# Three embedding blocks and sixteen idle products at the start of a hybrid encoder step, and one store on another queue

## The chip, the core and the metric

The kernel runs on one core of a Trainium2 chip. The metric is the time of one launch on the device in microseconds (us), lower is better. TensorE (PE in the profile) multiplies matrices, VectorE (DVE), ScalarE (ACT) and GpSimd (POOL) work element by element, and SyncE (SP) issues most of the transfers.

## The reference

One inference step of a one-layer encoder on 1024 prompt rows and 32 decode rows, all in float32, `D_MODEL` 1024. Cut to what is computed:

```python
h = rmsnorm(x, g_mix)
q, k, v, cb, cc, cx, ga, gc = jnp.split(h @ w_in, SPLITS, axis=-1)
y_attn = attend(q, k, v).reshape(b, t, SB_WIDTH) @ w_attn_out   # stick-breaking, 8 heads x 64
conv_out, new_buf = causal_conv(cc * cx, conv_buf, conv_w)      # width 3, 512 channels
y_conv = (cb * conv_out) @ w_conv_out
x = x + (sigmoid(ga) * y_attn + sigmoid(gc) * y_conv) @ w_o
x = x + square(relu(rmsnorm(x, g_ffn) @ w_up)) @ w_down         # 4 * D_MODEL wide
x = x + sigmoid(rmsnorm(x, g_ple) @ w_ple_gate) * (p @ w_ple)   # p: 256 features per row
y = rmsnorm(x, g_final)
```

The term `p @ w_ple`, the embedding, hangs on no other part of the step: its inputs are `p` (1056 x 256) and `w_ple` (256 x 1024).

## The kernel before

Activations lie feature-major: a block is 128 features by T = 1056 rows (1024 prompt, 32 decode). Each f32 product is made of three fp32r products: a tensor is cast to a high part on ScalarE (`h`), and the low part is the difference, on VectorE (`l`); TensorE adds high x high, high x low and low x high in one PSUM group.

The stages in order:

1. *Loads and first gates.* Two gate weights (`raw_i`) and the input `xf` are loaded on SyncE's queue. `first_gates` makes the first four gate blocks in 16 groups of 24 products, 264 columns each (`products`, lines 202 to 204). `prepare_plain` casts the weights (`load_w`, lines 97 and 98), `parts_x` makes the high and low parts of the scaled input (lines 328 and 141).
2. *Input projections.* Twelve more sets by a seven-product scheme (`seven`): gates 4 to 9, then cc, cx, cb, q, k, v twice. What follows a set (`follow`) runs as side generators beside the next set. For `cb` that is `conv_gate`: it casts the gated convolution to `cvh` on ScalarE (line 567), stores it to `cvd` (line 568), subtracts for the low part (570) and stores that (571).
3. *Attention.* 64 steps of 128 queries each: eight heads (p, j), with eight steps i = 0 to 7 over a growing key length of 128 (i + 1). A step has scores (`scores`, TensorE lines 799 and 800, sigmoid on ScalarE, masking on GpSimd), a running product on VectorE (`left_over`, line 817), transposes on TensorE with copies out by ScalarE and subtractions by VectorE (`flip`, lines 853 to 857), and every second step the sum over values (`gather`, line 872). The steps are staggered over four loop turns in the hand-written `ORDER`. Between them TensorE is given *filler units*: gates 10 to 15 (four units each, `gate_unit` and `last_gates`), then the eight embedding blocks (one unit each, `embed_unit`, 18 products with three column slices of 352; the last two blocks are cut otherwise). START = 6 units run ahead of the attention, FILL in it.
4. *Branch projections, merge, output projection, MLP, embedding gate and final norm.*

`pace` spreads FILL over the steps. Each step has a load of the other engines, an `own` time of TensorE, and the filler is what lies between them; four times 1.25 are added for splitting the embedding's inputs (`p_parts`) and weights (`embed_weights`):

```python
unit = (FILL * 2.92 + sum(own)) / sum(load)
part = [max(0.0, unit * v - o) for v, o in zip(load, own)]
part = [x * FILL / sum(part) for x in part]
...
load[next(n for n, e in enumerate(ends) if e > FILL - 11 + more)] += 1.25
```

Inside the blocks of `tc.manual_schedule(engines=MM)` the order on TensorE, VectorE, ScalarE and GpSimd is the order in which the code issues; SyncE's order is chosen by the framework. Blocks of T columns share one pool of 34 buffers (`blk`), raw weights a pool of four (`wraw`).

Of the kernel before, what the change touches and what calls it, by code (L numbers as in the profile page):

```python
# [9 lines left out]
F32 = mybir.dt.float32  # L10
F32R = mybir.dt.float32r
# [4 lines left out]
P = 128  # L16
D = 1024
KD = D // P
# [18 lines left out]
TW = 400  # L37
# [1 line left out]
AT1 = (5, 4, 6, 7, 8, 12)  # L39
AT_IN = (4, 8, 10, 12, 14, 18)  # L40
EARLY_GATES = 10
FILL = 26.0
ORDER = "LSAFBFG"
START = 6
MM = {mybir.EngineType.Activation, mybir.EngineType.PE, mybir.EngineType.DVE, mybir.EngineType.Pool}
# [3 lines left out]
def tile_step(  # L49
# [8 lines left out]
    nc = tc.nc  # L58
# [229 lines left out]
            )  # L288

    near_, far_, whole_ = slice(0, TQ), slice(TQ, TH), slice(0, TH)  # L290
    n_ = base["g"]
    raws["i0"] = [raw_w(w_in, n_, KD, "i0_0")]
    load_x(0, near_)
# [24 lines left out]
    rs = blk("rs")  # L318
    ssq = cpool.tile([P, 9], F32, name="ssq")
    rst = cpool.tile([P, 9], F32, name="rst")  # L320

    def parts_x(h, c, fs=(0, 2, 4, 6, 1, 3, 5, 7)):
        for f in fs:
# [236 lines left out]
    def conv_gate(nb, m):  # L560
        scaled(m)
        yield
        dve(m, m, cst.pop(("y", nb)), op=ALU.mult)
        for _ in range(8 if nb % 2 else 3):
            yield
        h = blk(f"cvh{nb}", F32R)
        nc.scalar.copy(h, m)
        nc.sync.dma_start(cvd[nb, 0], h.bitcast(F32))
        yield
        dve(m.bitcast(F32R), m, h.bitcast(F32), op=sub)  # L570
        nc.sync.dma_start(cvd[nb, 1], m)
        yield
# [17 lines left out]
    def first_gates():  # L590

        m, late = [blk(f"sg{n}") for n in range(2)], []

        def out(s_, i, t):
            p_ = late.pop(0)
            r = m[2 * s_ + i]
            nc.scalar.copy(r[:, quarters[t]], p_)
            if t == (3, 1)[s_]:
                nc.sync.dma_start(gd[2 * s_ + i], r)

        order = [(0, i, t) for t in range(4) for i in range(2)]
        order += [(1, i, t) for h in ((2, 3), (0, 1)) for i in range(2) for t in h]
        for n, (s_, i, t) in enumerate(order):
            if n == 0:
                prepare_plain("i0", 0)
                parts_x(0, near_)
                prepare_plain("i0", 1)
            elif n in (1, 3):
                parts_x(n // 2, far_ if n == 1 else whole_)
            elif n == 8:  # L610
                m.extend(blk(f"sg{n}") for n in (2, 3))
            w, c = ws[f"i{s_}"], t // 2 + 1
            a, b = (("A11", "A12"), ("A21", "A22"))[i]
            late.append(products(f"g{s_}{i}{t}", ((w[a], f"B1{c}"), (w[b], f"B2{c}")), quarters[t % 2]))
            if n:
                out(*order[n - 1])
            if n + 1 == len(order):
                out(*order[n])
            if n == 4:
                side.append(sums_x())  # L620
            elif n in (6, 7):
                prepare_plain("i1", n - 6)
            elif n == 8:
                fetch_in(2)
                side.append(prepare("i2"))
            elif n == 12:
                fetch_in(3)
            yield
# [76 lines left out]

    def p_fetch():
        for i in range(2):
            pwr.append(wraw.tile([P, 4, 2, P], F32, tag="raw", name=f"raw_pw{i}"))
            nc.sync.dma_start(pwr[i], w_ple[:, 4 * i : 4 * i + 4])
        for f in range(2):  # L710
            praw.append(blk(f"pr{f}"))
            nc.sync.dma_start(praw[f], pT[f])
# [4 lines left out]
        pl.append(l)  # L717

    def embed_weights(i):
        h, l = (blk(f"pw{i}{x}", F32R, [P, 4, 2, P]) for x in "hl")  # L720
        nc.scalar.copy(h, pwr[i])
        dve(l, pwr[i], h.bitcast(F32), op=sub)
        pw.append((h, l))

    def embed_unit(n):


        def body(w):
            if 3 <= n < 7:
                conv_parts(n - 3)  # L730
            wh, wl = (x[:, n % 4] for x in pw[n // 4])
            e = blk(f"em{n}")
            cols = ts if n < KD - 2 else tt[:2]
            for c in cols:
                ps = group(f"ps_pw{n}{c.start}", c.stop - c.start)
                for k in range(2):
                    nc.tensor.matmul(ps, wh[:, k, :], ph[k][:, c], start=k == 0, stop=False)
                    nc.tensor.matmul(ps, wh[:, k, :], pl[k][:, c], start=False, stop=False)
                    nc.tensor.matmul(ps, wl[:, k, :], ph[k][:, c], start=False, stop=k == 1)
                nc.scalar.copy(e[:, c], ps)  # L740
                if c is cols[-1]:
                    nc.sync.dma_start(ed[n][:, : c.stop], e[:, : c.stop])
                yield 1 / 3
            if n < KD - 2:
                return
            b = n - (KD - 2)
            tb = slice(2 * TW + b * P, 2 * TW + b * P + P)
            wh, wl = (x[:, 2:4] for x in pw[1])
# [12 lines left out]
        return lambda: None, lambda raw: None, body, (0, 1), 1  # L761
# [184 lines left out]
        return load, body  # L946

    units = [gate_unit(n, 1 if n == 13 else 2) for n in range(EARLY_GATES, 14)] + [last_gates(14)]
    units += [embed_unit(n) for n in range(KD)]
    work = feed(units)  # L950
    done = 0

# [11 lines left out]

    with tc.manual_schedule(engines=MM):
        nc.scalar.preload_act_table_set("sqrt_and_others")
        run(first_gates())
        for s_ in range(2, len(SETS)):
            nm, n = SETS[s_]
            if s_ == 2:  # L970
                side.append(after(1, stats_x()))
            elif s_ == 4:
                nc.scalar.preload_act_table_set("sigmoid_and_others")
            if s_ + 1 < len(SETS):
                side.append(prepare(f"i{s_ + 1}", AT_IN))
# [958 lines left out]
```

## Time and profile before

| | |
|---|---|
| median of 3 runs | 1548.17 us (1547.71 to 1549.49) |
| the profiled execution | 1548.24 us |
| its span, first to last instruction | 1546.5 us |
| TensorE busy | 1524.3 us (99%) |
| VectorE busy | 1061.1 us (69%) |
| ScalarE busy | 756.7 us (49%) |
| transfers | 269.10 MB, mean 174 GB/s |

In a timeline row stand the start, the duration, the engine, the line, the operation, out <- in, the shape, the count, and in brackets the idle time ahead of it and what ended it. A wait row has who waited for whom: the total in us, how many times, the longest. A row of the windows has the stretch, its length, the busy time of PE, PEld (weight loads), DVE, ACT and POOL with their counts, the granted clock, the share of DMA and GB/s. The ends of TensorE's products are modelled and overlap the next product, so the rate is read from the distance between starts. A busy share of TensorE is not its share of peak.

### The profile page before, as it was taken

How to read it: one execution, taken by the hardware profiler on the slowest of the kernel's cores; microseconds unless marked ns; L12 is line 12 of the kernel's file. 1: busy time of each engine (PE TensorE's matmuls, PEld its weight loads, DVE VectorE, ACT ScalarE, POOL GpSimd, SP SyncE). 2: the span in 40 equal slices, each digit the busy share in tenths (PEclk: the TensorE clock that was granted, in tenths of full speed). 3: DMA queues.
4: the chain of work that ended last, by engine and by line, in shares of the span. 5: the costliest groups of instructions: out<-in, count | busy, mean ns of one | idle time of the engine just before them, and what ended most of it. 6: DMA issues, size and time to landing. Idle time of an engine off the chain costs nothing.

```text
span 1546.5 us, 29356 instructions
## 1 busy us (share of the span) xinstructions
PE 1524.3 (99%) x11786; PEld 1509.7 (98%) x11786; DVE 1061.1 (69%) x1398; ACT 756.7 (49%) x1384; POOL 344.5 (22%) x290
## 2 busy tenths in 40 slices
PE   8999999999999999999999999999999999999997
PEld 7999999999899999999999999999999999999997
DVE  7544776666678887766577555545577986789856
ACT  6643344443566775333355555555543334434656
POOL 1222332220211115001312222221020221013352
PEclk9999999999999999999999999999999999999999
DMA  6532145544635466234453344344786897583443
GB/s 226 202 115 72 40 177 205 196 146 110 216 106 155 158 228 241 85 136 169 161 190 144 141 152 147 132 146 154 272 310 203 279 334 243 193 280 112 141 134 111
DMA packets 111559, 269.10 MB, mean 174 GB/s; under 512 B 13472, under 2 KB 29216, under 8 KB 111424
## 3 DMA queue, kind: packets, MB, share of 16 engines
q1 hardware_dynamic: 111280, 267.21, 50.6%
q8 instruction: 92, 1.51, 0.4%
q14 instruction: 43, 0.35, 0.1%
q10 hardware_dynamic: 144, 0.03, 0.0%
HBM read 186.46 MB, written 80.73 MB: 173 GB/s over the span
## 4 chain that ended last, share of the span: by engine, by line
PE 91%; DVE 4%; ACT 2%; issue 1%; DMA 1%; POOL 0%; SPq 0%; POOLq 0%; DVEq 0%; ACTq 0%
PE ps_dn L1467 7%; PE ps_dn L1466 7%; PE ps_dn L1468 7%; PE ps_A11u L203 4%; PE ps_A11u L204 4%; PE ps_A11u L202 4%; PE ps_A11i L204 3%; PE ps_A11i L202 3%; PE ps_A11i L203 3%; PE av L872 2%; PE ps_wo L107 2%; PE ps_wo L106 2%; PE ps_wo L108 2%; PE ps_S1u L203 2%; PE ps_S1u L202 2%; PE ps_S1u L204 2%
## 5 line engine op out<-in xcount | busy, mean ns | idle before, releaser
L1467 PE MATMUL ps_dn<-fl,whi_dn 128*128 128x264 f32 x896 | 254.8, 284 | 0.1
L1468 PE MATMUL ps_dn<-fh,wlo_dn 128*128 128x264 f32 x896 | 254.8, 284 | 0.0
L1466 PE MATMUL ps_dn<-fh,whi_dn 128*128 128x264 f32 x896 | 254.7, 284 | 0.0
L1467 PEld LDWEIGHTS ps_dn<-fl,whi_dn 128*128 128x128 f32 x896 | 168.5, 188 | 0.3 <-DVE fl L1375 0.3
L1466 PEld LDWEIGHTS ps_dn<-fh,whi_dn 128*128 128x128 f32 x896 | 168.7, 188 | 0.0
L1468 PEld LDWEIGHTS ps_dn<-fh,wlo_dn 128*128 128x128 f32 x896 | 168.6, 188 | 0.0
L189 POOL TENSOR_TENSOR s_i<-raw_i,raw_i 128x512 f32<-128x512 f32 x30 | 40.7, 1358 | 229.0 <-DVE slS_i L152 196.1
L1359 DVE TENSOR_TENSOR wlo_dn<-raw_dn,whi_dn 128x1024 fp32r<-128x1024 f32 x40 | 71.2, 1780 | 25.7 <-ACT whi_dn L1353 25.6
L817 DVE TENSOR_TENSOR_SCAN r<-r 128x128 f32<-128x128 f32 (+3 forms) x64 | 86.6, 1353 | 2.2 <-POOL r L810 2.0
L1353 ACT CAST whi_dn<-raw_dn 128x1024 fp32r<-128x1024 f32 x40 | 42.1, 1052 | 94.0 <-PE ps_dn L1467 79.7
L189 POOL TENSOR_TENSOR s_u<-raw_u,raw_u 128x512 f32<-128x512 f32 x30 | 44.3, 1476 | 186.6 <-DVE slS_u L152 157.9
L1408 POOL TENSOR_TENSOR c<-c,rs 128x528 f32<-128x528 f32 x16 | 26.7, 1668 | 244.1 <-DVE c L1475 122.5
L1375 DVE TENSOR_TENSOR fl<-mr,fh 128x1056 fp32r<-128x1056 f32 x56 | 69.7, 1246 | 4.1 <-ACT fh L1370 4.1
L810 POOL TENSOR_SCALAR_AFFINE_SELECT r<-r 128x128 f32<-128x128 f32 x64 | 25.9, 406 | 204.7 <-ACT r L803 204.7
L152 DVE TENSOR_TENSOR slS_i<-s_i,shS_i 128x512 fp32r<-128x512 f32 x45 | 35.2, 787 | 51.8 <-ACT shS_i L150 51.7
L202 PE MATMUL ps_A11u<-T,shS_u 128*128 128x264 f32 x240 | 68.5, 285 | 0.0
L202 PE MATMUL ps_A11i<-T,shS_i 128*128 128x264 f32 x240 | 68.5, 285 | 0.0
L204 PE MATMUL ps_A11i<-T,slS_i 128*128 128x264 f32 x240 | 68.4, 285 | 0.0
L203 PE MATMUL ps_A11u<-T,shS_u 128*128 128x264 f32 x240 | 68.4, 285 | 0.0
L204 PE MATMUL ps_A11u<-T,slS_u 128*128 128x264 f32 x240 | 68.3, 284 | 0.0
L203 PE MATMUL ps_A11i<-T,shS_i 128*128 128x264 f32 x240 | 68.2, 284 | 0.0
L857 DVE TENSOR_TENSOR at<-pa,at 128x512 fp32r<-128x512 f32 (+2 forms) x96 | 51.0, 550 | 19.6 <-ACT at L856 18.8
(462 smaller groups left out, 5604.8 us busy)
## 6 DMA issues: line engine op xcount, KB each, us to landing
raw_dn<-in_w_down_dram SPq DMA_DIRECT2D x56, 512.0 KB, 4.8
raw_i<-in_w_in_dram SPq DMA_DIRECT2D x34, 512.0 KB, 4.5
mr<-mdT SPq DMA_DIRECT2D x32, 528.0 KB, 5.7
raw_u<-in_w_up_dram SPq DMA_DIRECT2D x32, 512.0 KB, 3.6
mdB<-m SPq DMA_DIRECT2D x48, 264.0 KB, 2.4
mr<-mdB SPq DMA_DIRECT2D x24, 528.0 KB, 5.9
s<-gd SPq DMA_DIRECT2D x16, 528.0 KB, 5.3
mdT<-ta SPq DMA_DIRECT2D x32, 264.0 KB, 2.1
```

The source lines that it names most:

```text
L189: f()
L202: nc.tensor.matmul(p_, wh[:, k, :], o[:, 0, c], start=new and n == 0, stop=False, **on)
L203: nc.tensor.matmul(p_, wh[:, k, :], o[:, 1, c], start=False, stop=False, **on)
L204: nc.tensor.matmul(p_, wl[:, k, :], o[:, 0, c], start=False, stop=z, **on)
L817: nc.vector.tensor_tensor_scan(rev, rev, rev, 1.0, ALU.mult, ALU.bypass)
L857: nc.vector.tensor_tensor(al, pt[:, :nb, :], ah.bitcast(F32), op=ALU.subtract)
L1353: nc.scalar.copy(hi, dws[u])
L1359: dve(lo, raw, hi.bitcast(F32), op=sub)
L1375: dve(l, mraw.pop(v), opd[v].bitcast(F32), op=sub)
L1466: nc.tensor.matmul(ps, hi[:, j, :], oh, start=j == 0, stop=False)
L1467: nc.tensor.matmul(ps, hi[:, j, :], ol, start=False, stop=False)
L1468: nc.tensor.matmul(ps, lo[:, j, :], oh, start=False, stop=j == NP_ - 1)
```

## The change

Three embedding blocks (n = 0, 1, 2) leave the attention's fillers and are made by a new function, `first_embeds`, ahead of the first gates. Their loads stand ahead of the first gate weight on SyncE's queue: `w_ple` for the three blocks in two pieces and `p` in six column pieces (1.47 MB). Ahead of their 54 products stand WARM = 16 products of `ones` with itself, whose result nobody reads. Their PSUM groups are emptied inside `first_gates`, by ScalarE for the first and third column slice and by VectorE for the second. FILL goes from 26 to 23. The later loads and casts of `w_ple` take the five remaining blocks; `p` is loaded and cast again for them. In `conv_gate` the store of the high part is issued from ScalarE's queue in place of SyncE's. What is computed stays the same.

```diff
-FILL = 26.0
+FILL = 23.0
+FIRST_EMBEDS = 3
+WARM = 16
...
+    NE = FIRST_EMBEDS
+    pw_first = wraw.tile([P, NE, 2, P], F32, tag="raw", name="raw_pw_first")
+    p_first = [blk(f"pf{f}") for f in range(2)]
+    nc.sync.dma_start(pw_first[:, :1], w_ple[:, :1])
+    for c in ts:
+        for f in range(2):
+            nc.sync.dma_start(p_first[f][:, c], pT[f][:, c])
+        if c is ts[0]:
+            nc.sync.dma_start(pw_first[:, 1:], w_ple[:, 1:NE])
     n_ = base["g"]
     raws["i0"] = [raw_w(w_in, n_, KD, "i0_0")]
...
+    def first_embeds():
+
+        wu = gps.tile([P, TW], F32, tag="g", name="warm")
+        for _ in range(WARM):
+            nc.tensor.matmul(wu[:, :P], ones, ones, start=True, stop=True)
+        wh, wl = (blk(f"pwf{x}", F32R, [P, NE, 2, P]) for x in "hl")
+        h, l = ([blk(f"pf{x}{f}", F32R) for f in range(2)] for x in "hl")
+        e = [blk(f"em{n}") for n in range(NE)]
+        late = []
+
+        def low_w(n):
+            dve(wl[:, n], pw_first[:, n], wh[:, n].bitcast(F32), op=sub)
+
+        def out():
+            n, c, ps = late.pop(0)
+            (nc.vector.tensor_copy if c is ts[1] else nc.scalar.copy)(e[n][:, c], ps)
+            if c is ts[-1]:
+                nc.sync.dma_start(ed[n], e[n])
+
+        nc.vector.tensor_copy(wh[:, 0], pw_first[:, 0])
+        low_w(0)
+        for i, c in enumerate(ts):
+            for f in range(2):
+                nc.scalar.copy(h[f][:, c], p_first[f][:, c])
+            if i == 0:
+                nc.scalar.copy(wh[:, 1:], pw_first[:, 1:])
+            for f in range(2):
+                dve(l[f][:, c], p_first[f][:, c], h[f][:, c].bitcast(F32), op=sub)
+            if i == 0:
+                low_w(slice(1, NE))
+            for n in range(NE):
+                ps = group(f"ps_pw{n}_{i}")
+                for k in range(2):
+                    nc.tensor.matmul(ps, wh[:, n, k, :], h[k][:, c], start=k == 0, stop=False)
+                for k in range(2):
+                    nc.tensor.matmul(ps, wl[:, n, k, :], h[k][:, c], start=False, stop=False)
+                for k in range(2):
+                    nc.tensor.matmul(ps, wh[:, n, k, :], l[k][:, c], start=False, stop=k == 1)
+                late.append((n, c, ps))
+        return out
...
-        nc.sync.dma_start(cvd[nb, 0], h.bitcast(F32))
+        nc.scalar.dma_start(cvd[nb, 0], h.bitcast(F32))
...
                 prepare_plain("i0", 0)
-                parts_x(0, near_)
+                for _ in range(NE):
+                    embed_out()
+                parts_x(0, near_, (0, 2, 4, 6))
+                for _ in range(NE):
+                    embed_out()
+                parts_x(0, near_, (1, 3, 5, 7))
                 prepare_plain("i0", 1)
             elif n in (1, 3):
+                if n == 1:
+                    for _ in range(NE):
+                        embed_out()
                 parts_x(n // 2, far_ if n == 1 else whole_)
...
-            pwr.append(wraw.tile([P, 4, 2, P], F32, tag="raw", name=f"raw_pw{i}"))
-            nc.sync.dma_start(pwr[i], w_ple[:, 4 * i : 4 * i + 4])
+            pwr.append(wraw.tile([P, 3, 2, P], F32, tag="raw", name=f"raw_pw{i}"))
+            nc.sync.dma_start(pwr[i][:, 1 - i :], w_ple[:, 3 + 2 * i : 5 + 3 * i])
...
-    units += [embed_unit(n) for n in range(KD)]
+    units += [embed_unit(n) for n in range(NE, KD)]
...
         nc.scalar.preload_act_table_set("sqrt_and_others")
+        embed_out = first_embeds()
         run(first_gates())
```

More of the change, by code (lines that the diff above doesn't have):

```diff
@@ L719, in embed_weights @@
     def embed_weights(i):
-        h, l = (blk(f"pw{i}{x}", F32R, [P, 4, 2, P]) for x in "hl")
-        nc.scalar.copy(h, pwr[i])
-        dve(l, pwr[i], h.bitcast(F32), op=sub)
+        h, l = (blk(f"pw{i}{x}", F32R, [P, 3, 2, P])[:, 1 - i :] for x in "hl")
+        nc.scalar.copy(h, pwr[i][:, 1 - i :])
+        dve(l, pwr[i][:, 1 - i :], h.bitcast(F32), op=sub)
         pw.append((h, l))
@@ L730, in body @@
                 conv_parts(n - 3)
-            wh, wl = (x[:, n % 4] for x in pw[n // 4])
+            wh, wl = (x[:, n - (3 if n < 5 else 5)] for x in pw[n >= 5])
             e = blk(f"em{n}")
@@ L747, in body @@
             tb = slice(2 * TW + b * P, 2 * TW + b * P + P)
-            wh, wl = (x[:, 2:4] for x in pw[1])
+            wh, wl = (x[:, 1:3] for x in pw[1])
             ps = group(f"ps_pt{b}", 2 * P)
```

## The prediction

> **What bounds the kernel now.** I read the page's totals and chain first, then who TensorE waited for, then the timelines of the three places that the change touches: the opening, the first convolution stores, and the attention.
>
> ```profile
> span 1546.5 us, 29356 instructions
> PE 91%; DVE 4%; ACT 2%; issue 1%; DMA 1%; POOL 0%; SPq 0%; POOLq 0%; DVEq 0%; ACTq 0%
> ```
>
> The chain that ended last is TensorE for 91%. Moving TensorE work pays only where it fills a hole, and only if the place it leaves can run shorter. TensorE's waits over the whole run, those of the attention:
>
> ```profile
> PE z L799 <- ACT r L803: 1.0, 2, 0.5
> PE pa L853 <- DVE r L817: 1.0, 2, 0.8
> ```
>
> The attention shows only 2 us of such waits, so today its fillers are paid in full. The largest hole is the opening (start, duration, engine and line):
>
> ```profile
> 0.90 0.17 DVE L75 MEMSET ones<- 128x128 f32 x1 [0.90 <-PEq L1910]
> 1.24 1.96 SPq L286 DMA_DIRECT2D x<-in_xf_dram  x4
> 4.42 1.04 ACT L97 CAST whi_i<-raw_i 128x1024 fp32r<-128x1024 f32 x1 [1.90 <-DMA raw_i<-in_w_in_dram]
> 5.93 0.59 PE L202 MATMUL ps_g<-B,whi_i 128*128 128x264 f32 x1 [5.93 <-ACT B L328]
> 7.18 0.59 PE L203 MATMUL ps_g<-B,whi_i 128*128 128x264 f32 x1 [0.66 <-DVE B L141]
> 10.20 0.42 PE L204 MATMUL ps_g<-B,wlo_i 128*128 128x264 f32 x1
> 10.42 0.32 PE L202 MATMUL ps_g<-B,whi_i 128*128 128x264 f32 x1
> 11.55 0.28 PE L202 MATMUL ps_g<-B,whi_i 128*128 128x264 f32 x1
> 11.67 0.28 PE L203 MATMUL ps_g<-B,whi_i 128*128 128x264 f32 x1
> 12.11 0.39 PE L204 MATMUL ps_g<-B,wlo_i 128*128 128x264 f32 x1 [0.15 <-DVE wlo_i L98]
> ```
>
> TensorE starts at 5.93. Until 10.42 its products stand 0.22 us apart (10.20, 10.42), later 0.12 (11.55, 11.67): the array runs at about half speed for its first 4.5 us. From 5.93 to 11.67 there are 26 products, worth 26 x 0.121 = 3.15 us at full speed, so 12.11 - 3.15 = 8.96 us are lost by 12.11. One wait follows in the same stage:
>
> ```profile
> 33.47 0.39 PE L204 MATMUL ps_g<-B,wlo_i 128*128 128x264 f32 x1 [0.63 <-DVE wlo_i L98]
> ```
>
> That makes 9.6 us.
>
> **The opening, after.** The sixteen products multiply `ones` by itself in plain f32. The nearest rows are nine products of the same form, and two rows of an embedding block:
>
> ```profile
> L390 PE MATMUL pr<-dg,ones x18: 195/275/377, 83.7 to 85.6; 128*128 128x128 f32 x16, 128*128 128x32 f32 x2
> 534.31 0.32 PE L738 MATMUL ps_pw<-p0l,pw0h 128*128 128x352 f32 x1
> 534.96 0.33 PE L739 MATMUL ps_pw<-p1h,pw0l 128*128 128x352 f32 x1
> ```
>
> Nine products are 18 instructions in 1.9 us, two each, 0.11 us apart at full speed. Slowed as in the opening (0.22 / 0.121 = 1.8) one takes 0.20. Sixteen are 32 instructions from 1.2 us on, when `ones` is set. If the slow stretch lasts 4.5 us again (5.93 to 10.42), 22.5 instructions run slowly until 5.7 and 9.5 fast: done at 6.75. If it lasts 3.2 (7.18 to 10.42), done at 6.2; if it outlasts them, at 1.2 + 32 x 0.20 = 7.6. I take 6.75, the longer stretch being the one counted from the first product. The Trainium skill, "TensorE: Matmul & The Clock Gate", Part 1, puts the warm-up at about 3.4 us of activity in a window that runs freely of the kernel's start; by it the slow stretch would end anywhere from 4.6 to 8.0, an estimate from that page, and the sum below would move by -0.5 to +0.9 us. The trace's 3.2 and 4.5 lie inside that.
>
> Three blocks of 18 products follow. Their rows are 0.16 us apart (four steps from 534.31 to 534.96), so 54 x 0.161 = 8.7 us, and the gates begin at 15.45. Do the inputs come in time?
>
> ```profile
> vecT<-in_vecs_dram ACTq DMA_DIRECT2D x1, 26.0 KB, 3.8
> x<-in_xf_dram SPq DMA_DIRECT2D x8, 264.0 KB, 5.4
> 6.00:9.00 3.00, 2.34 (x9) 2.04 (x10) 2.75 (x6) 2.31 (x6) 0.00 (x0) 1.00 1.05 396
> L740 ACT COPY em<-ps_pw x22: 452/454/506, 524.3 to 579.8; 128x352 f32<-128x352 f32 x18, 128x400 f32<-128x400 f32 x4
> 10.70 3.41 ACT L328 ACTIVATE B<-x,vecT 128x264 fp32r<-128x264 f32 x8
> ```
>
> The smallest load took 3.8 us to land, so the first weight block (131 KB) is there by 4.6; the two 180 KB input pieces behind it, at 396 GB/s, by 5.5; with a cast of about 0.45 the first block can run at 6, under the cover of the idle products. The eight new loads move 1.47 MB, 3.8 us at that rate, and take SyncE's queue 8 x 0.49 = 3.9 us of issuing ahead of the first gate weight. All first-stage loads land 3.8 us later, the gate weight at 8.2 (4.42 + 3.8). ScalarE then casts it (1.04), empties three PSUM groups (1.4) and makes eight parts (8 x 0.43); VectorE follows with its eight parts and three copies. Laid end to end the first four parts are ready near 13 and the last near 16, against 15.45 and about 16.9 when they are used (half a group of 24 products later). That cover is some 1 us; if it is gone, 1 us is added. The 0.63 wait at 33.47 comes in a stage where ScalarE and VectorE have moved less than TensorE; I keep 0.3 of it. Sum: 6.75 + 8.7 + 0.3 - 9.6 = **+6.15 us**, bounds +5.3 (6.2, no wait) and +8.4 (7.6, wait kept, inputs 1 us late). The later `ed` stores on SyncE's queue have nothing urgent behind them.
>
> **The convolution store.** In the sets of input projections:
>
> ```profile
> 193.40 1.08 ACT L567 CAST cvh<-m_i 128x1056 fp32r<-128x1056 f32 x1 [2.22 <-DVE m_i L563]
> 196.89 0.38 SPq L568 DMA_DIRECT2D cvd<-cvh  x1
> 196.89 5.33 DMA cvd<-cvh
> 202.31 1.07 ACT L567 CAST cvh<-m_i 128x1056 fp32r<-128x1056 f32 x1 [6.09 <-DMA cvd<-cvh]
> 205.03 0.39 PE L202 MATMUL ps_A11i<-B,whi_i 128*128 128x264 f32 x1 [1.61 <-DVE m_i L248]
> ```
>
> The cast ends at 194.48, but SyncE, busy with earlier work in its order, issues the store at 196.89; it lands 5.33 us later, ScalarE's next cast waits 6.09 us for that buffer, and everything behind the cast, up to TensorE at 205.03, is late by 1.61. Issued from ScalarE's own queue the store goes 2.4 us earlier; 2.4 is more than 1.61, so the whole wait goes: **-1.6 us**. Four issues of about 0.4 us now stand in ScalarE's order ahead of the casts and PSUM copies, an engine that waits 2.2 us in this very row. Bounds: -1.6, and +1.6 should the issues hold up PSUM copies as long again as today's wait.
>
> **The attention, with 23 units.** Three units of 18 products leave: -8.7 us if TensorE stays the bound. The eight-step stretches, one head each (length, then busy TensorE, weight loads, VectorE):
>
> ```profile
> 416.50:442.60 26.10, 26.10 (x211) 24.13 (x209) 17.34 (x24) 13.92 (x38) 3.66 (x8) 1.00 0.36 108
> 442.60:463.60 21.00, 21.00 (x169) 20.46 (x168) 19.52 (x27) 14.48 (x34) 3.37 (x9) 1.00 0.42 119
> 463.60:484.60 21.00, 21.00 (x168) 20.45 (x167) 19.16 (x26) 14.12 (x33) 2.90 (x8) 1.00 0.46 139
> 484.60:508.00 23.40, 23.40 (x187) 22.77 (x186) 18.83 (x26) 14.14 (x33) 2.35 (x8) 1.00 0.47 141
> 508.00:532.10 24.10, 23.97 (x181) 22.71 (x179) 22.16 (x28) 17.74 (x40) 4.78 (x8) 1.00 0.57 190
> 532.10:553.90 21.80, 21.13 (x151) 20.14 (x149) 18.90 (x26) 15.36 (x37) 3.24 (x9) 1.00 0.62 196
> ```
>
> By `pace`'s own formula the units per eight steps go from 4.15, 2.67, 2.67, 2.67, 3.61, 3.61, 2.67, 2.67 (1.26 behind) to 3.75, 2.33, 2.33, 2.33, 3.66, 2.77, 2.33, 2.33 (1.15). At 2.9 us a unit (18 x 0.161) the third and fourth stretches shrink by 1.0 to 20.0 against VectorE's 19.5 and 19.2, the seventh to 20.8. The sixth shrinks by 2.4 to 21.7. It holds the low parts of the embedding's inputs and weights:
>
> ```profile
> 507.83 1.26 DVE L114 TENSOR_TENSOR p0l<-pr,p0h 128x1056 fp32r<-128x1056 f32 x1 [0.22 <-ACT p0h L113]
> 516.54 1.22 DVE L722 TENSOR_TENSOR pw0l<-raw_pw,pw0h 128x1024 fp32r<-128x1024 f32 x1 [0.26 <-ACT pw0h L721]
> ```
>
> `pace` reserves time for these four at units 15 to 18, written as FILL - 11 on; with FILL at 23 that is 12 to 15, while they still run at 15 to 18, since only later units left. So the added time lands mostly in the fifth stretch, and the first cast (1.26, now just ahead of the sixth) moves into the sixth. The weight casts shrink to half and three quarters (0.6 and 0.9 for 1.22 each); the second falls behind step 48, into the seventh. VectorE's sixth stretch: 22.16 + 1.26 - 0.6 - 1.2 = 21.6 by that, up to 22.5 if the last cast stays.
>
> VectorE has left TensorE unhurt with 1.5 us of room in a stretch (21.0 against 19.52). If it needs those 1.5 us, the third, fourth, sixth and seventh stretches fall short by 1.0, 0.7, 2.3 and 0.5: 4.5 us lost. If it needs none, only the sixth is short, by 0.8. I take 2.4, about half way, as no row shows less room than 1.5 and the stretches can lend to each other. Saved: 8.7 - 2.4 = **-6.3 us**, bounds -4.2 and -7.9.
>
> Sum: +6.15 - 1.6 - 6.3 = -1.75 us. The profiled execution took 1548.24 us (span 1546.5 and 1.7 around it), within 0.1 of the median of three runs, 1548.17. Forecast: 1548.24 - 1.75 = **1546.5 us**.
>
> **Rivals.** *The attention pays in full* (chance 0.25): VectorE keeps up with no room to spare, as its waits shrink when TensorE's transposes come sooner, and the opening is at its lower bound: +5.3 - 1.6 - 7.9 = -4.2, 1544.0 us. For it: 17.34 busy of 26.10 in the second stretch. Against it: 92% busy in the third.
>
> *The attention does not shorten* (0.10, the slow side): VectorE's idle time there is its own order (cast of ScalarE, then its subtraction, then the scan), so every stretch keeps its length and TensorE waits where the fillers stood. Then +6.15 - 1.6 = +4.55, 1552.8 us. It decides as soon as less than about 1.5 us is saved. Against it: TensorE busy 21.00 of 21.00, so the length is TensorE's now.
>
> *The idle products open nothing* (0.08): the array stays slow until about 10.4 whatever ran before. They end at 7.6, then 2.8 us of embedding run at half speed, 1.4 lost: +8.4, in sum +0.5, 1548.7 us.
>
> *ScalarE's store waits in its own queue* (0.05): a DMA issue can wait for an earlier transfer, as this row of SyncE's waits in the first 40 us shows:
>
> ```profile
> SPq L88 <- DMA raw_i<-in_w_in_dram: 6.2, 1, 6.2
> ```
>
> On ScalarE such a wait holds the PSUM copies: the 1.6 stays and up to 6.2 less 2.2 is added: 1548.1 to 1552.1 us.
>
> **How the numbers follow.** The forecast has the remaining 0.52. About 0.2% (3.1 us) is what a measurement of this kernel can tell from no change. Faster by more: nearly all of the first rival and a little of the forecast's low end, 0.30. Slower by more: the second rival and the tail of the last, 0.12. Same: 0.58. The range runs from the first rival with the 508 us stretch unhurt (1543.2) to the forecast with opening and attention both near their bad bounds (1548.24 + 8.4 - 1.6 - 4.2 = 1550.8), cut to 1550.6; it leaves out most of the second rival.
>
> **What would show it.** Right: idle products from 1.2 to about 6.8, embedding products 0.16 apart from about 7, gates from about 15.5 without a hole; no 6.09 wait at the second convolution cast and no 1.61 before the next product; the attention shorter by about 6 us, with a few us of new TensorE waits for the scan or the low parts, most of them near the sixth stretch. Wrong: embedding products 0.3 apart, gates starting after 16.5, a ScalarE wait at the store, or an attention as long as before.

## The result and the profile after

The changed kernel takes 1552.87 us (median of 10 runs, 1551.89 to 1553.5) against 1548.26 (10 runs, 1547.71 to 1550.32) for the kernel before in the same comparison: ratio 1.0027, 95% interval [1.0017, 1.0037]. The forecast was 1546.5 with a range up to 1550.6, so the change is slower where a gain of 1.75 us was expected, and outside the range. Its profiled execution took 1553.01 us, 4.77 more than the 1548.24 of before.

The page's span, and the chain that ended last (shares by engine):

```profile
span 1551.3 us, 29450 instructions
PE 90%; DVE 5%; ACT 2%; issue 1%; DMA 1%; POOL 0%; SPq 0%; DVEq 0%; POOLq 0%; ACTq 0%
```

TensorE still carries the chain. Where the 4.8 us arose is read from the starts of the same products in both timelines. The table gives for every kernel of this study how much later (+) or earlier (-) than in the kernel before, in us, the named product started in the profiled execution.

| kernel | first input set | first scores | attention's last `av` | second branch (`ps_oa`) | first `ps_pg` | last `ps_pg` | end |
|---|---|---|---|---|---|---|---|
| before, at | 56.72 | 392.09 | 586.36 | 631.14 | 1431.80 | 1538.72 | 1546.52 |
| changed | +8.17 | +6.00 | +1.78 | +2.56 | +2.65 | +4.31 | +4.78 |
| changed again | +8.25 | +6.09 | +1.84 | +2.60 | +2.68 | +4.19 | +4.76 |
| e1 store alone | -0.08 | -1.56 | -1.90 | -1.91 | -2.26 | -2.25 | -2.26 |
| e8 store, idle products | -0.12 | -1.61 | -1.96 | -1.97 | -2.36 | -2.33 | -2.17 |
| e4 GpSimd sums out | +5.96 | +3.53 | -0.65 | -0.10 | -0.02 | +0.11 | +1.05 |
| e10 sums later | +6.69 | +5.39 | +1.26 | +2.71 | +2.12 | +2.11 | +2.13 |
| e6 10 idle products | +7.84 | +5.67 | +1.63 | +1.70 | +1.76 | +3.35 | +3.29 |
| e5 no idle products | +9.30 | +7.12 | +3.04 | +3.12 | +3.18 | +3.33 | +4.26 |
| e7 26 units | +8.11 | +5.89 | +4.49 | +4.61 | +3.90 | +3.82 | +3.85 |
| e3 later due units | +7.84 | +5.63 | -0.78 | +1.31 | +1.24 | +1.29 | +1.42 |
| e9 and more cover | +8.23 | +6.03 | -0.56 | +0.21 | +0.54 | +0.54 | +0.61 |
| e13 gates on VectorE | +7.87 | +5.70 | +1.49 | +1.63 | +2.48 | +2.60 | +2.59 |
| e11 combined | +5.62 | +4.32 | -2.39 | -1.96 | -2.81 | -2.76 | -2.69 |

So the opening costs 8.17, the stretch with the convolution stores gives 2.2 back, the attention 4.2, the branch projections lose 0.8, the last step 1.7, and what stands behind the last product 0.5 more. What TensorE waited for, over the whole changed run (who for whom, total us, times, longest):

```profile
PE pa L913 <- DVE r L877: 2.1, 4, 0.8
PE z L859 <- ACT r L863: 1.8, 4, 0.5
PE ps_g L206 <- DVE wlo_i L100: 1.6, 1, 1.6
PE pas L1094 <- DVE oT L837: 1.4, 1, 1.4
```

Before, the first two stood at 1.0 each, the third at single waits of 0.6, and the fourth was not there.

**The opening.** TensorE, ScalarE and VectorE rows of the changed kernel's timeline (start, duration):

```profile
1.12 6.49 PE L337 MATMUL warm<-ones 128*128 128x128 f32 x32 [1.12 <-DVE eps_t L79]
7.36 0.57 PE L366 MATMUL ps_pw<-pfh,pwfh 128*128 128x352 f32 x2
10.40 1.05 ACT L99 CAST whi_i<-raw_i 128x1024 fp32r<-128x1024 f32 x1 [0.73 <-DMA raw_i<-in_w_in_dram]
16.28 0.29 PE L204 MATMUL ps_g<-B,whi_i 128*128 128x264 f32 x1
34.47 5.91 DVE L143 SCALAR_TENSOR_TENSOR x<-x,vecT,x 128x528 f32<-128x528 f32 x4
40.31 1.21 DVE L100 TENSOR_TENSOR wlo_i<-raw_i,whi_i 128x1024 fp32r<-128x1024 f32 x1
41.58 0.39 PE L206 MATMUL ps_g<-B,wlo_i 128*128 128x264 f32 x1 [1.56 <-DVE wlo_i L100]
```

The idle products end at 7.36, the embedding products follow without a hole, and the gates begin at 16.28. But at 41.58 TensorE loses 1.56 us to a low weight that stands behind four sums in VectorE's order; these take 5.91 us. In the kernel before they took 4.87, and GpSimd's four sums for the next set ran from 23.92 on. VectorE's sums and GpSimd's last before (first two rows), then GpSimd's first and last after:

```profile
27.41 4.87 DVE L141 SCALAR_TENSOR_TENSOR x<-x,vecT,x 128x528 f32<-128x528 f32 x4
28.71 1.64 POOL L189 TENSOR_TENSOR s_i<-s_i,raw_i 128x512 f32<-128x512 f32 x1
32.45 1.54 POOL L191 TENSOR_TENSOR s_i<-raw_i,raw_i 128x512 f32<-128x512 f32 x1 [31.08 <-DMA raw_i<-in_w_in_dram]
37.50 1.64 POOL L191 TENSOR_TENSOR s_i<-s_i,raw_i 128x512 f32<-128x512 f32 x1
```

Before, GpSimd had finished at 30.35, in the middle of VectorE's sums; now it works until 39.14, beside nearly all of them (34.47 to 40.38).

**The convolution store.** ScalarE's rows:

```profile
201.27 1.08 ACT L619 CAST cvh<-m_i 128x1056 fp32r<-128x1056 f32 x1 [2.26 <-DVE m_i L615]
202.38 0.33 ACTq L620 DMA_DIRECT2D cvd<-cvh  x1
206.63 1.08 ACT L619 CAST cvh<-m_i 128x1056 fp32r<-128x1056 f32 x1 [2.04 <-DVE m_i L622]
```

The store is issued right behind its cast, and the next cast waits for its input (2.04), not for a buffer (6.09).

**The attention.** The stretches of eight steps as before (length, then busy PE, PEld, DVE, ACT, POOL):

```profile
398.10:422.20 24.10, 21.29 (x170) 19.48 (x170) 18.90 (x28) 13.71 (x31) 7.75 (x24) 1.00 0.70 233
447.40:468.50 21.10, 20.82 (x163) 19.74 (x162) 19.52 (x27) 14.50 (x34) 4.82 (x9) 1.00 0.48 144
488.70:513.80 25.10, 24.30 (x191) 23.42 (x191) 19.75 (x27) 13.51 (x32) 4.15 (x9) 1.00 0.45 128
513.80:536.40 22.60, 21.73 (x168) 20.45 (x167) 20.15 (x26) 15.52 (x36) 6.28 (x8) 1.00 0.45 129
536.40:557.70 21.30, 20.59 (x151) 19.58 (x150) 20.64 (x29) 15.52 (x37) 4.18 (x9) 1.00 0.81 232
```

The first, which took 24.4 before, hardly shrinks; the third not at all; the fifth grows from 23.4 to 25.1. The last 12 us of the first show why it could not shrink (a window before, one after, and TensorE's wait in the latter):

```profile
405.20:417.20 12.00, 11.18 (x85) 10.17 (x84) 11.81 (x16) 6.54 (x15) 1.32 (x3) 1.00 0.62 190
410.80:422.80 12.00, 9.73 (x74) 8.67 (x73) 11.78 (x15) 5.96 (x12) 2.15 (x3) 1.00 0.45 142
421.89 0.55 PE L1094 MATMUL pas<-ident,ss 128*128 128x128 f32 x3 [1.45 <-DVE oT L837]
```

VectorE, 18.4 busy of 24.4 on average, was busy 11.8 of 12.0 us in the last half of this stretch already before. With less filler TensorE now waits there, at the transposes of the decode rows, the sample (`pas`), for `oT`, which VectorE makes at the end of that stretch. In the fifth stretch TensorE has 191 products where it had 187, and one wait:

```profile
489.77 0.66 PE L913 MATMUL pa<-ident,r 128*128 128x128 f32 x4 [0.79 <-DVE r L877]
```

**The branch projections.** VectorE's low weights of the last two blocks, GpSimd's multiplication of a gate beside the second, and TensorE's wait for it, in the changed kernel:

```profile
618.88 0.69 DVE L100 TENSOR_TENSOR wlo_oc<-raw_oc,whi_oc 128x512 fp32r<-128x512 f32 x1 [0.80 <-ACT whi_oc L99]
625.05 2.47 POOL L966 TENSOR_TENSOR s<-s,rs 128x1056 f32<-128x1056 f32 x1 [2.66 <-DVE mg L995]
625.38 2.69 DVE L100 TENSOR_TENSOR wlo_oc<-raw_oc,whi_oc 128x512 fp32r<-128x512 f32 x1 [0.37 <-ACT whi_oc L99]
628.12 0.43 PE L110 MATMUL ps_oc<-cv,wlo_oc 128*128 128x352 f32 x1 [0.44 <-DVE wlo_oc L100]
```

The same instruction takes 0.69 alone and 2.69 when GpSimd's multiplication has begun 0.33 ahead of it. TensorE's product starts 0.76 after the one ahead of it, where 0.16 is the rule. In the kernel before the same low weight took 1.77, and TensorE did not wait for it.

**The last step.** Windows near the end, two of before and then two of after (the column behind POOL is the granted clock):

```profile
1538.00:1540.00 2.00, 1.00 (x9) 0.79 (x7) 1.31 (x4) 1.97 (x3) 0.00 (x0) 1.00 0.05 22
1542.00:1544.00 2.00, 0.00 (x0) 0.00 (x0) 0.90 (x3) 0.72 (x1) 0.00 (x0) 0.77 0.11 43
1538.00:1540.00 2.00, 1.83 (x12) 1.72 (x13) 1.19 (x4) 1.98 (x4) 0.00 (x0) 0.82 0.56 205
1540.00:1542.00 2.00, 2.00 (x12) 2.00 (x11) 1.60 (x7) 1.29 (x3) 0.00 (x0) 0.50 0.03 8
```

Before, the granted clock falls only when the last product is done (at 1543.07). After, it is 0.50 from 1539.29 to 1542.70, while the last products run; 3.41 us at half clock lose 1.7. Whether this belongs to the change is asked in e12.

### The profile page after: what moved, and what is told of

It is laid out like the page before. It is cut to its first block, busy times and chain, and to the rows that moved or that the text cites. A ratio compares the mean times of both kernels' runs of the same rounds, so it can differ in the third digit from the quotient of the medians.

```text
span 1551.3 us, 29450 instructions
## 1 busy us (share of the span) xinstructions
PE 1530.5 (99%) x11818; PEld 1515.0 (98%) x11818; DVE 1067.1 (69%) x1410; ACT 757.0 (49%) x1388; POOL 350.0 (23%) x290
## 4 chain that ended last, share of the span: by engine, by line
PE 90%; DVE 5%; ACT 2%; issue 1%; DMA 1%; POOL 0%; SPq 0%; DVEq 0%; POOLq 0%; ACTq 0%
PE ps_dn L1529 7%; PE ps_dn L1528 7%; PE ps_dn L1527 7%; PE ps_A11u L205 4%; PE ps_A11u L204 4%; PE ps_A11u L206 4%; PE ps_A11i L204 4%; PE ps_A11i L206 4%; PE ps_A11i L205 4%; PE ps_wo L108 2%; PE ps_wo L110 2%; PE ps_wo L109 2%; PE av L932 2%; PE ps_S1u L205 2%; PE ps_S1u L204 2%; PE ps_S1u L206 2%
## 5 line engine op out<-in xcount | busy, mean ns | idle before, releaser
L870 POOL TENSOR_SCALAR_AFFINE_SELECT r<-r 128x128 f32<-128x128 f32 x64 | 33.1, 518 | 194.3 <-ACT r L863 194.3
L1431 ACT CAST fh<-mr 128x1056 fp32r<-128x1056 f32 x56 | 60.1, 1073 | 5.6 <-DMA mr<-mdB 5.6
```

Source lines behind the costliest of these rows:

```text
L1431: nc.scalar.copy(h, mraw[v])
```

## The experiments

Two causes were to be told apart at each place: an engine that has no room left, or an order that spoils the room there is. The kernel before had a median of 1548.84 to 1549.68 in the comparisons below and 1548.26 in the first, so the ratios to it are what compares. The changed kernel's is 1.0027, and 1.0022 when measured again (e12).

**e1, the store alone**, in the kernel before:

```diff
-        nc.sync.dma_start(cvd[nb, 0], h.bitcast(F32))
+        nc.scalar.dma_start(cvd[nb, 0], h.bitcast(F32))
```

> The kernel before with one line changed: the high part of the convolution is stored from ScalarE's queue. Theory (the store waited behind other work in SyncE's order): the 6.09 us wait of the second convolution cast and the 1.61 us TensorE wait after it go, 1.4 to 1.8 us faster, the opening and the attention as before. Rival (the 1.5 us that the changed kernel gained there came from other buffers being handed out after the new blocks, not from the queue): the 1.61 stays and the time is that of before, within 0.3 us.

Measured: 1546.23 us against 1548.9 (33 runs), ratio 0.9984 [0.9975, 0.9992].

```profile
193.31 1.08 ACT L567 CAST cvh<-m_i 128x1056 fp32r<-128x1056 f32 x1 [2.23 <-DVE m_i L563]
194.42 0.33 ACTq L568 DMA_DIRECT2D cvd<-cvh  x1
198.68 1.08 ACT L567 CAST cvh<-m_i 128x1056 fp32r<-128x1056 f32 x1 [2.05 <-DVE m_i L570]
```

The store is issued at 194.42 instead of 196.89, the next cast begins at 198.68 instead of 202.31, and the input sets end 1.56 earlier. The queue was the cause. This one line is worth 2.3 us by the end, more than the 1.4 to 1.8 expected, and beats both kernels; where the 0.7 behind the first scores comes from is open.

**e4, GpSimd's four sums for the first set by the seven-product scheme left out** in the changed kernel. Three fills with a constant stand in their place and are done by 2.8 us:

> The changed kernel with GpSimd's four sums for the third weight pair (set i2) left out and three memsets in their place, so that GpSimd reads nothing while VectorE makes the sums of the input; what that set computes is then not the reference's. Theory (GpSimd's sums hold up VectorE, whose four sums take 5.9 us in place of 4.9): the four take under 4 us, the 1.6 us TensorE wait at 39.7 us shrinks below 0.3, 1.3 us or more faster than the changed kernel. Rival (VectorE is late there because the first weights and inputs came late): VectorE's four sums stay near 5.9 us and the wait stays.

Measured: 1551.56, ratio 1.0018 [1.0009, 1.0027]. VectorE's sums:

```profile
33.06 2.80 DVE L143 SCALAR_TENSOR_TENSOR x<-x,vecT,x 128x528 f32<-128x528 f32 x4
```

2.80 instead of 5.91, no wait for `wlo_i`, and the first set 2.21 earlier (0.38 of it from an earlier start of the gates). So GpSimd's sums beside them slow VectorE's, and that, not the later data, made the wait. The ratio fell only from 1.0027 to 1.0018; the last column of the table shows a profiled end 3.7 earlier, but that was the fastest of runs that spread from 1549.28 to 1554.64.

**e10, the sums of x one gate group later** in the changed kernel, so that the low weight stands ahead of them:

```diff
-            if n == 4:
+            if n == 5:
                 side.append(sums_x())
```

> The changed kernel with the sums of x begun one gate group later, so that VectorE's program has the low weight of the second gate pair ahead of its four sums and not behind them. If the extra 2 us of the opening are VectorE's order (low weight behind four sums that GpSimd's sums stretch to 5.9 us): the wait of 1.6 us at 39.7 us goes, the first product of the first set comes at 62.7 to 63.5 us instead of 64.89, and the median falls by 1.3 to 2.2 us. If the opening is longer because its data come later whatever the order: the wait moves to another tile near it and the first set comes at 64.5 to 65 us.

Measured: 1549.96 against 1548.84, ratio 1.0008 [1.0, 1.0017].

```profile
8.15 0.59 PE L366 MATMUL ps_pw<-pfh,pwfh 128*128 128x352 f32 x2 [0.59 <-ACT pwfh L358]
37.95 2.10 DVE L100 TENSOR_TENSOR wlo_i<-raw_i,whi_i 128x1024 fp32r<-128x1024 f32 x1 [4.32 <-ACT whi_i L99]
41.34 2.80 DVE L143 SCALAR_TENSOR_TENSOR x<-x,vecT,x 128x528 f32<-128x528 f32 x4
67.12 0.39 PE L204 MATMUL ps_S1i<-T,shS_i 128*128 128x264 f32 x1 [0.62 <-ACT shS_i L152]
```

In the opening the clock record opens at 4.57 in this execution, 2.1 us earlier than in the first, and yet the gates begin at 16.39: the second piece of the embedding weights holds TensorE until 8.15. Later the low weight comes first (slowed itself, 2.10 instead of 1.21), the sums run after GpSimd in 2.80, and the wait of 1.56 is gone: first set 1.48 earlier, as expected. But two waits of 0.62 and 0.37 appear at 67 us, for what is now made too late, by the first scores only 0.6 of it is left, and by the first `ps_oa` nothing (+2.71 against +2.56). Of the 2.65 by which its end comes earlier than the changed kernel's, 2.1 arise behind the first `ps_pg`, above all in the last step, which ran at full clock in this profile.

**e6, 10 idle products, the first weights in one transfer**, and **e5, no idle products**, both in the changed kernel:

```diff
-WARM = 16
+WARM = 10
...
-    nc.sync.dma_start(pw_first[:, :1], w_ple[:, :1])
+    nc.sync.dma_start(pw_first, w_ple[:, :NE])
```

> The changed kernel with 10 idle products instead of 16 and the first embedding weights in one transfer. If TensorE, held by its idle products until 7.36 us and then never waiting, sets when the gates begin: idle products end near 5.1 us, a few embedding products run slow until the clock record opens near 6.7, and the gates begin at 14.7 to 15.3 us instead of 16.28; the first set comes 0.5 to 1.5 us earlier. If x and the gate weights set it: holes of over 0.3 us between the products between 10 and 17 us and the first set within 0.3 us of 64.89.

> The changed kernel without idle products. If TensorE's clock opens some 5 us after its first product whatever that computes: the embedding products begin at 5.1 us, run slow until 9.7 to 10.9 us, and the gates begin at 16 to 17 us, within 0.8 us of the changed kernel's 16.28, so that the idle products are worth under 0.8 us. If only a longer dense run of work opens it (before's record opens at 10.49): the gates come after 17 us and the median rises by 1 us or more.

Measured: e6 1550.9, ratio 1.0012 [1.0003, 1.0021]; e5 1552.3, ratio 1.002 [1.0011, 1.0028]. The first embedding product of e6, and two of e5:

```profile
6.08 0.94 PE L364 MATMUL ps_pw<-pfh,pwfh 128*128 128x352 f32 x2 [0.33 <-ACT pfh L354]
4.71 0.66 PE L363 MATMUL ps_pw<-pfh,pwfh 128*128 128x352 f32 x1 [4.71 <-ACT pfh L353]
7.23 0.79 PE L367 MATMUL ps_pw<-pfl,pwfh 128*128 128x352 f32 x2
```

e6's gates begin at 15.39: 0.9 of the 1 to 1.6 expected, because the inputs are there only at 6.08. At the first set 0.33 of it is left, where 0.5 to 1.5 was expected. Half is lost by 20 us, most of it ahead of a product at 18.91 that comes 0.41 after the one before. And the low weight of 41.58 comes only 0.32 earlier, because VectorE's four sums, beside GpSimd's, take 6.95. e5's products start at 4.71 and stand 0.3 apart until 12.4, where the clock record opens, 7.7 us after the first; the gates begin at 17.75, as in the second case. The idle products are worth 1.1 us at the first set, but the median did not rise by the 1 us of that case: behind the attention this profile lost less, with no fall of the clock ahead of the last products.

**e8, the store alone and 12 idle products, no embedding blocks**, in the kernel before:

> The kernel before with the store from ScalarE's queue and 12 idle products ahead of the gates, no embedding products. If the opening without embeddings is set by the data and VectorE: the clock record opens some 4 us earlier than 10.49, the holes between the first gate products grow by what the products get shorter, and the first set comes within 0.5 us of the store alone (56.64). If the slow clock itself costs: it comes 1.3 to 2 us earlier, and the median with it.

Measured: 1546.26, ratio 0.9982 [0.9974, 0.9991]; e1 had 1546.23. The clock record opens at 5.83 instead of 12.68, and the first set comes 0.04 earlier.

```profile
7.21 0.39 PE L203 MATMUL ps_g<-B,whi_i 128*128 128x264 f32 x1 [0.79 <-DVE B L141]
12.07 0.39 PE L204 MATMUL ps_g<-B,wlo_i 128*128 128x264 f32 x1 [0.76 <-DVE wlo_i L98]
```

At 12.07 the second weight is as late as at 12.11 before. The opening without embeddings is set by when VectorE has the inputs and weights ready; the slow clock was hidden in it.

**e7, 26 units** in the changed kernel: three units are made twice, so the attention has its old fill.

> The changed kernel with FILL at 26 again: three embedding units (blocks 3, 4, 3) are made twice in the attention, so that TensorE has as much filler there as before. Theory (the attention's new waits, about 4.7 us in all, come from the smaller filler): TensorE's waits for pas, pa and z return to about 3.5 us, the attention to 194.5 to 195.5 us, the kernel some 4 to 4.5 us slower than the changed one. Rival (they come from other buffers or from where the attention starts): the waits of 1.4 us at pas and 1.0 in the fifth stretch stay, and the kernel is 8 us or more slower than the changed one.

Measured: 1552.09, ratio 1.0018 [1.0009, 1.0026]. Its waits in the attention are those of before again:

```profile
PE z L859 <- ACT r L863: 1.0, 2, 0.5
PE pa L913 <- DVE r L877: 0.8, 1, 0.8
```

From first scores to last `av` it takes 192.9 us, the changed kernel 190.1: 8.7 us of products fewer bought 2.8 there, and nothing in the median. So the new waits do come from the smaller filler, but the 4 to 4.5 us expected for the whole kernel were a miss.

**e3, the extras past unit 15** in the changed kernel, where they stood with 26 units, and **e9**, which adds cover at the sample's step:

```diff
-                load[next(n for n, e in enumerate(ends) if e > FILL - 11 + more)] += 1.25
+                load[next(n for n, e in enumerate(ends) if e > 15 + more)] += 1.25
...
-            load.append(max(v, 1.6) + 3.0 * (n == 6) + 0.5 * (n == 4))
+            load.append(max(v, 1.6) + 5.0 * (n == 6) + 0.5 * (n == 4))
```

> The changed kernel with the four extra loads of pace placed at units 15 to 18 in place of FILL - 11 on, where the casts of the embedding's inputs and weights run. Theory A (filler put 3 units early makes TensorE wait for VectorE in the fifth and sixth eight-step stretch): the waits there of 1.0, 0.7 and 0.5 us go, 1 to 2 us faster than the changed kernel. Theory B (VectorE has too little room wherever filler is taken): the waits move to other steps, within 0.5 us of the changed kernel.

> The kernel with the later due units (extras past unit 15 instead of 12), and besides 5.0 us instead of 3.0 of planned cover at the step in which the sample's products stand. If the 1.66 us wait for the transposed output at 420 us is a question of too few units beside VectorE's queue there: it goes or falls under 0.5 us, and the end of the attention comes 0.8 to 1.5 us earlier than with the later due units alone (av 585.6). If VectorE's own work sets that stretch: the wait stays within 0.3 us, one unit more only moves there from the other stretches, and the end of the attention stays or comes later.

Measured: e3 1549.45 against 1548.9, ratio 1.0001 [0.9992, 1.001]; e9 1549.47 against 1548.84, ratio 1.0003 [0.9994, 1.0012]. The fifth to seventh stretch of e3, and e9's wait for the scan:

```profile
488.30:508.90 20.60, 19.81 (x157) 19.05 (x155) 18.83 (x25) 12.25 (x29) 3.70 (x9) 1.00 0.33 99
508.90:531.30 22.40, 22.40 (x179) 21.86 (x178) 19.07 (x26) 14.72 (x36) 2.95 (x8) 1.00 0.55 168
531.30:555.20 23.90, 23.40 (x176) 22.61 (x175) 22.83 (x31) 17.41 (x40) 2.98 (x9) 1.00 0.68 206
PE pa L913 <- DVE r L877: 2.3, 3, 1.6
```

With the extras where the splitting really runs, the fifth stretch is 4.5 us shorter than in the changed kernel, mostly because products moved: it has 157 instead of 191, the sixth and seventh 179 and 176 instead of 168 and 151. Over the last four stretches together the same filler takes 97.3 us instead of 99.5. The waits of 0.5 and 0.3 in the sixth go; the 0.8 in the fifth stays. The attention takes 187.9 us in all. Of the 2.56 by which it ends earlier 1.25 is left at `ps_oa`, because TensorE now waits 1.5 for a low weight in the branch projections; the rest of the lower ratio is the last step, at full clock here.

The wait for `oT` at 420 us goes in e9, but another of 1.6, for the scan, takes its place, and the attention ends 0.2 later than in e3. There VectorE's own work is the bound: the end is the rival's, though the rival had the wait itself stay.

**e13, the convolution gates multiplied on VectorE** in the changed kernel:

```diff
-                sgs["c"] = gate_values(8 + n, pool)
+                sgs["c"] = gate_values(8 + n, dve)
```

> The changed kernel with the convolution gates' multiplication by the row scale (six of 128x1056) on VectorE instead of GpSimd. If the loss in the branch projections is VectorE slowed by GpSimd's multiplication at the same time (low weight 2.69 us instead of 0.69): every wlo_oc takes 0.6 to 1.3 us, TensorE's waits for wlo_oc go, and the first ps_oa comes 0.8 to 1.1 us earlier than 633.70. If it is VectorE's own queue: the multiplications now stand in it, the low weights come later, and ps_oa comes at 633.7 or later.

Measured: 1550.52 against 1549.68, ratio 1.0008 [0.9999, 1.0017].

```profile
621.93 0.69 DVE L100 TENSOR_TENSOR wlo_oc<-raw_oc,whi_oc 128x512 fp32r<-128x512 f32 x1
```

All six low weights take 0.7 us and TensorE's waits for them go. From the last `av` to `ps_oa` the kernel now loses 0.14 to the kernel before, not 0.78: collision, not VectorE's queue. Whether a collision costs depends on where TensorE is. e6, whose attention ends 0.15 earlier, has the same low weight at 2.59, does not wait for it, and loses 0.07. And of the 0.93 that e13 has at `ps_oa`, 0.17 is left at the first `ps_pg`.

**e11, all of it together** (e6, e10, e9 and e13):

> The changed kernel with what the runs so far bought, all at once: 10 idle products and one transfer of the first embedding weights, the sums of x one gate group later, extras past unit 15 and 5.0 us of cover at the sample's step, and the six GpSimd multiplications of the convolution gates on VectorE. If the parts add (opening: 1.48 from the order and 0.9 from the idle products, now that no wait for the low weight swallows it; attention as with the later due units; no wait in the branch projections): first set at 62.3 to 62.9 us, the branch projections' second half (first ps_oa) at 628.5 to 629.5 us, and a median of 1545.5 to 1547, 2 to 3 us under the kernel before and near the store alone. If the gains are one slack counted several times: first set after 63.2, first ps_oa after 630.5, median 1548 or more.

Measured: 1546.32 against 1549.68, ratio 0.998 [0.9971, 0.9989]. The first set is at 62.34, `ps_oa` at 629.18, as expected if the parts add. In the same comparison e8, the store and idle products alone, had 1546.26, so nothing is gained: with these orders mended, the moved blocks cost 5.9 us up to the first scores against e1 (+4.32 and -1.56) and save 6.4 in the attention (187.6 and 193.9). They pay for themselves and hardly more. No run has the new orders without the moved blocks, so what the orders would be worth alone is open.

**e12, the changed kernel again:**

> The changed kernel once more, unchanged. If the 1.7 us that its profiled execution lost behind the last step (clock record at 0.5 from 1539.29 to 1542.7 us, while products still ran) is part of the change: the record falls again ahead of the last products and the median is 1552.5 to 1553.2. If it is where the record's 3.41 us steps happen to fall in an execution: the profile may show no fall before 1542 us and an end near 1549.5, and the median lies 0.5 to 1.5 us lower, at 1551.4 to 1552.4. The waits of the opening (1.6 at 39.7 us) and of the attention (pas for oT near 1.5) come back in both cases.

Measured: 1552.46 against 1549.43, ratio 1.0022 [1.0013, 1.0031], a difference of 3.0 us where the first comparison had 4.6. The record falls again, as in the first case, and the median is just below that case's range. The profile repeats the first to 0.12 us at every place of the table; the clock falls at 1539.74, not at 1539.29. So both profiles of this kernel have the slow step ahead of the last products, the one of the kernel before has it behind them. How many of the runs without a profile it strikes stays open. Where runs of the two kernels have the same mean clock, 0.997, 0.998 or 0.999, their spans in this comparison differ by 3.0 (1551.25 and 1548.28), 3.2 (1550.65 and 1547.46) and 3.35 (1549.7 and 1546.35); within each kernel the clock makes 1.5 to 2. So at equal clock the change costs 3.0 to 3.4 us. The runs of the kernel before at 0.997 are 1.9 longer than those at 0.999, about what one slow step costs. This suggests, but no profile shows, that the step strikes that kernel too, and that the 1.7 is chance more than part of the change.

## Why the prediction was wrong

*The step that failed.* Two terms of the sum were mis-sized, both close to their bad bounds: the opening cost 8.17 instead of 6.15, and the attention gave 4.2 instead of 6.3. With the store's stretch (-2.2) that makes 1550.0 us, a loss of 1.8 but still inside the range. What carried the time out of it are the 3.0 us behind the attention, which the sum has at nothing: 0.8 in the branch projections, 0.1 up to the first `ps_pg`, 1.7 in the last step, 0.5 behind the last product. Even the 3.0 to 3.4 us of equal clocks (e12) are more than the 2.4 that the range allows above 1548.24. By the sum itself, +6.15 and -6.3, the moved blocks were worth 0.15 us; the forecast gain was the store's.

*The opening: +6.15 forecast, +8.17 measured; the mechanism held, two terms were mis-sized.* The gates began at 16.28, not 15.45. The idle products ended at 7.36, not 6.75, as the slow stretch outlasted nearly all of them (record open at 6.71, 5.6 after the first product, where the sum took 4.5), and the 54 products took 8.9, not 8.7. A faster clock would have helped by 0.4 at most: over the profiles with all sixteen products the gates begin at 15.90 to 16.39, and in e10, where it opened at 4.57, the second weight piece, cast at 7.35 in the changed kernel, held the products instead. That these inputs would be there in time was said of the first block only; the others were not looked at. The Trainium skill's free-running window, from which the prediction drew 4.6 to 8.0 as an estimate ("TensorE: Matmul & The Clock Gate", Part 1), holds for six of the eight profiles that have all sixteen products, up to 7.16 us (e12); e10's 4.57 and e13's 4.36 lie just ahead of it. So does the shorter of the two lengths that the prediction put inside: 3.2 from 1.2 on ends at 4.4. Between e13 and e12 the first set moved by only 0.4. The 0.63 wait of which 0.3 was kept became 1.56: 1.3 more. The argument for keeping little, that VectorE had moved less than TensorE, looked at VectorE alone. Its sums share the time with GpSimd's, whose place is set by when its weight lands; e4 and e10 show it. The gate weight's cast came at 10.40, not 8.2; TensorE's own lateness covered that.

The prediction counted the slow clock of the first 4.5 us among the 9.6 us lost. e8 shows that by itself it cost nothing there: with the clock open at 5.83 the first set comes only 0.04 earlier, as VectorE's parts are no earlier.

*The convolution store: -1.6 forecast.* Right: the 6.09 and the 1.61 are gone, and e1 measures -1.56 at the first scores. The changed kernel gains 2.2 over the same stretch; the 0.6 more is not explained.

*The attention: -6.3 forecast, -4.2 measured, at the bad bound.* The third, fourth, sixth and seventh stretches lost together what the 2.4 allowed: by their units they should have shrunk by 1.0, 1.0, 2.4 and 1.0, and shrank by -0.1, 0.9, 1.5 and 0.6, short by 2.5 (the eighth gave 1.0 more than its units). Two steps failed. The first stretch is not among those for which a shortfall was worked out, so it counted with its full saving of 1.2; it shrank by 0.3, for the wait of 1.45 shown above. The fifth was expected to stay; it grew by 1.8, with a few products more and the wait of 0.8 for the scan. The prediction saw the extras that `pace` writes from FILL - 11 move and priced it only in the sixth; e3 shows that their place costs 2.2 over the last four stretches. With the extras put back the attention is 6.4 us shorter than before. That this is the forecast's figure is partly luck: the shortfalls lie in other stretches than it had them, the first among them.

*Not in the sum at all:* 0.8 in the branch projections (e13: the same collision of GpSimd and VectorE, in code that the change does not touch) and 1.7 in the last step (the clock; e12 leaves open how much of that is the change's). Where the 0.5 behind the last product comes from is open.

*The rivals.* None came true. The slow one, an attention that does not shorten, gave 1552.8, close to the result, but for another reason: two thirds of its saving came, and the rest was lost elsewhere. That the idle products open nothing is refuted: the record opens at 6.71, and without them at 12.4 (e5). That ScalarE's store waits in its own queue is refuted by the store rows: it is issued right behind its cast.

The Trainium skill, "SBUF — State Buffer", "Who interferes with whom", states that a VectorE instruction with two SBUF inputs and a GpSimd instruction that reads SBUF hold one read port against each other, the later one waiting for the whole of the other. The traces agree in the main: 0.69 became 2.69 beside GpSimd's 2.47, and 2.80 for four sums became 5.91. They are not a plain sum, though: VectorE's sums follow each other 0.68 us apart alone and GpSimd's 1.37, which makes 2.05, but beside each other both come every 1.72.

## What to carry to other kernels

Work that is moved ahead of a stage shifts everything behind it, so look at pairs of engines that by luck hardly overlapped before: list VectorE's two-input instructions and GpSimd's beside them at each place, and price a collision, not only a queue. An engine's average over a stretch says nothing of its last half; halve a stretch before its room is spent. A planner's constant that is written as a count from the end (FILL - 11) has to be moved by hand when units leave at the front. Measure the parts of a change apart: here one line, the store, was worth more than all the rest.

## What the runs showed of the hardware

The clock record changes only after whole steps of 3.41 us from where it opened (it stayed open for 1529.17, 1532.58, 1536.00 or 1539.41 us in the profiles, 448 to 451 times 3.413), and in the two executions of the changed kernel and in e6 it fell to 0.5 for one such step before the last products, although TensorE's single waits in that stage were at most 0.6 us. What decides is not shown: ahead of the fall in the changed kernel TensorE was busy 2.41 of 3.41 us (1535.88 to 1539.29), but in the kernel before 2.38 of 3.41 (1532.84 to 1536.25) passed at full clock. The record opened 3.2 (e13) to 7.7 us (e5) after the first product. The two longest, e5's and the 6.6 of e1, had holes of over 1 us among the first products, but with such a hole the kernel before took 4.6.
